# Linear attention on one core: the output of five of twelve groups written in 4 KB runs instead of 2 KB runs

## The chip, the cores and the metric

The kernel runs on one core of one Trainium2 chip. The metric is the device time of one execution in microseconds (us). Five runs of the kernel before took 127.0 to 128.05 us, median 127.46 us. A separate execution was profiled; its trace is what the views below show.

The names of the engines in the profile are PE (TensorE, matrix multiply), PEld (TensorE's weight loads), DVE (VectorE), ACT (ScalarE), POOL (GpSimd) and SP (SyncE, which here only issues transfers). "Sixteen DMA engines" are the engines that move the data; POOL and SP issue transfers to them through queues of their own.

## The reference, cut to what matters

Q, K and V are fp32 tensors of 8 x 12 heads, 512 rows and 64 columns.

```python
Q_feat = np.maximum(0, Q) + 1
K_feat = np.maximum(0, K) + 1
KV = np.einsum('bhkd,bhkv->bhdv', K_feat, V)            # 64 x 64 per head
K_sum = np.sum(K_feat, axis=2)                          # 64 per head
numerator = np.einsum('bhqd,bhdv->bhqv', Q_feat, KV)
denominator = np.einsum('bhqd,bhd->bhq', Q_feat, K_sum)
return numerator / (denominator[:, :, :, None] + 1e-10)
```

Inputs and output have 12.58 MB each, so 37.75 MB are read and 12.58 MB written.

## The kernel before, in words

**Layout of the inputs.** The 96 heads are taken in NG = 12 groups of eight. A group has two input blocks n. In a block, each of the 128 partitions holds C2 = 16 consecutive rows of 64 numbers, which is one run of 4 KB in memory, and 32 partitions make up one head. So a group is 2 blocks x 4 heads, and the 32 partitions 32b to 32b+31 belong to head b of each block. Loads go through POOL's queue and turn fp32 into bf16 on the way (all but the first K, which SP loads as fp32). Each K, V and Q load takes two groups (1024 KB in bf16) except for the first and the last ones, which take one.

**Steps of a group.** `k_features` and `q_features` add 1 and clip at 1 on VectorE. `v_blocks` copies V into a tile in which each head's rows stand apart (three copies on VectorE, one on ScalarE). `keys_values` makes KV and K_sum of the eight heads with 32 matmuls in two tiles of 64 columns, one tile for each block n, and ScalarE writes them as `kva`, a matrix of 128 x 130 for each b: block n = 0 in the upper 64 partitions and first 65 columns, block n = 1 in the rest, zeros elsewhere. `transposes` turns the Q features with 16 transposes, one for each row c of the 16 that a partition holds: the result has the 64 features of both blocks on its 128 partitions and the group's 128 row places as its columns. ScalarE copies it to `qt` in two halves of 8 rows.

**The output step.** `output` multiplies `qt` with `kva`. In the kernel before, each matmul takes 64 columns of weights: 32 row places of head b, and for each of them row c and row c + 8, which `qt` holds next to each other (`qt` is stored as row, place, half). Its 64 results therefore need 64 partitions, and a partition of the output holds 8 consecutive rows, a run of 2 KB. A pass h = 0, 1 handles heads 2h and 2h+1, one in each of the two 64-column tiles of TensorE. A pass fills two PSUM tiles `o_ps` (there are two buffers), eight matmuls each. For each `o_ps` VectorE takes the reciprocal of the denominators (L199) and multiplies (L200) into `o_sb`.

**Stores.** `store` sends one group's `o_sb`, 1024 KB. Groups 0 to 9 go through POOL as one transfer, groups 10 and 11 through SP as two transfers each, one per pass h, so that the first can go when pass 0 is done:

```python
o_dram = view(out, C)          # "(n p c) d -> p n c d" with c = 8: runs of 2 KB
...
if g < NG - 2:
    nc.gpsimd.dma_start(out=o_to, in_=o_sb)
    return
for h in range(2):
    nc.sync.dma_start(out=o_to[:, h:NP:2], in_=o_sb[:, h:NP:2])
```

**Order.** The order of all instructions is written out by hand. Each turn g of the main loop runs, on each engine's queue in this order: features of K, V's blocks, features of Q for group g; transposes of group g - 1; output of group g - 2; keys and values of group g; then a load two pairs ahead (every second turn), and the store of group g - 3. After the loop come group 11's steps, with output(9), output(10) and output(11), and the stores of groups 8 to 11. So POOL's queue holds loads and stores in one line, and TensorE's queue has, in each turn, transposes, output matmuls, key-value matmuls.

Of the kernel before, what the change touches and what calls it, by code (L numbers as in the profile page):

```python
# [8 lines left out]
FP32 = mybir.dt.float32  # L9
BF16 = mybir.dt.bfloat16  # L10
ALU = mybir.AluOpType

BANK = 512
# [6 lines left out]
def kernel(  # L20
# [18 lines left out]
    nc = tc.nc  # L39

    B, H, S, D = Q.shape
    P = 128
    C = 8
    C2 = 2 * C
    NPAIR = B * H * S // (P * C)
    NP = 4
    NG = NPAIR // NP
    D1 = D + 1
    W = 2 * D1

    def view(t, c):
        return t.flatten_outer_dims().rearrange("(n p c) d -> p n c d", p=P, c=c)
# [1 line left out]
    q_dram = view(Q, C2)  # L54
    k_dram = view(K, C2)
    v_dram = view(V, C2)
    o_dram = view(out, C)

    const = ctx.enter_context(tc.tile_pool(name="const", bufs=1))
    head_pool = ctx.enter_context(tc.tile_pool(name="head_pool", bufs=1))  # L60
# [2 lines left out]
    mid_pool = ctx.enter_context(tc.tile_pool(name="mid", bufs=3))  # L63
    out_pool = ctx.enter_context(tc.tile_pool(name="out_pool", bufs=OUT_BUFS))
    recip_pool = ctx.enter_context(tc.tile_pool(name="recip", bufs=4))
    psum_kva = ctx.enter_context(tc.tile_pool(name="psum_kva", bufs=2, space=bass.MemoryType.PSUM))
    psum = ctx.enter_context(tc.tile_pool(name="psum", bufs=2, space=bass.MemoryType.PSUM))
# [3 lines left out]
    NV = 3  # L71
# [4 lines left out]
    kva_diag = [const.tile([P, 4, 2, D1], BF16, name=f"kva_diag{i}") for i in range(NV)]  # L76
# [4 lines left out]
    qfs = {}  # L81
    qts = {}
    outs = {}

    def own(g):
        return slice(g % 2 * 2, g % 2 * 2 + 2)
# [24 lines left out]

    def store(g):
        o_sb = outs.pop(g)
        o_to = o_dram[:, g * NP : g * NP + NP]
        if g < NG - 2:
            nc.gpsimd.dma_start(out=o_to, in_=o_sb)  # L116
            return
        for h in range(2):
            nc.sync.dma_start(out=o_to[:, h:NP:2], in_=o_sb[:, h:NP:2])

    def feature(dst, src):
        nc.vector.tensor_scalar(  # L122
# [46 lines left out]

    def transposes(g):  # L170
        qf = qfs.pop(g)
        qt = mid_pool.tile([P, C, P, 2], BF16, name="qt")
        for half in range(2):
            qt_ps = psum_qt.tile([P, C, P], BF16, name="qt_ps")
            for c in range(C):
                nc.tensor.transpose(qt_ps[:, c, :], qf[:, half * C + c, :, :], identity)  # L176
            nc.scalar.copy(out=qt[:, :, :, half], in_=qt_ps)  # L177
        qts[g] = qt

    def output(g):  # L180
        kva = kva_diag[g % NV]
        qt = qts.pop(g)
        o_sb = out_pool.tile([P, NP, C, D], FP32, name="o_sb")
        for h in range(2):
            ops = [psum.tile([P, 2, BANK], FP32, tag="ps", name="o_ps") for _ in range(2)]
            for c in range(C):
                for j in range(2):
                    b = 2 * h + j
                    nc.tensor.matmul(  # L189
                        ops[c // 4][64 * j : 64 * j + 64, c // 2 % 2, (c % 2) * W : (c % 2) * W + W],  # L190
                        lhsT=qt[:, c, 32 * b : 32 * b + 32, :],
                        rhs=kva[:, b],
                        start=True,
                        stop=True,
                    )
            for i in range(2):
                cells = ops[i][:, :, 0 : 2 * W].rearrange("p b (c n x) -> p b c n x", n=2, x=D1)
                recip = recip_pool.tile([P, 2, 2, 2, 1], FP32, name="recip")
                nc.vector.reciprocal(out=recip, in_=cells[:, :, :, :, D:D1])  # L199
                nc.vector.tensor_tensor(  # L200
                    out=o_sb[:, h:NP:2, 4 * i : 4 * i + 4].rearrange(
                        "p n (b c) d -> p b c n d", b=2
                    ),
                    in0=cells[:, :, :, :, 0:D],
                    in1=recip.to_broadcast([P, 2, 2, 2, D]),
                    op=ALU.mult,
                )
        outs[g] = o_sb

    def clear(first, split, end):  # L210
# [7 lines left out]
    with tc.manual_schedule():  # L218
# [15 lines left out]
        for g in range(NG - 1):  # L234
            k_features(g)
            v_blocks(g)
            q_features(g)
            if g:
                transposes(g - 1)
            if g >= 2:  # L240
                output(g - 2)
            keys_values(g)
            if g % 2 and g // 2 + 2 < NG // 2:
                load_pair(g // 2 + 2)
            if g >= LAG:
                store(g - LAG)
        last = NG - 1
        k_features(last)
        v_blocks(last)
        transposes(last - 1)  # L250
        output(last - 2)
        q_features(last)
        keys_values(last)
        transposes(last)
        output(last - 1)
        output(last)
        for g in range(last - LAG, NG):
            store(g)
# [30 lines left out]
```

## Time and profile before

| | |
|---|---|
| median of five runs | 127.46 us (127.0 to 128.05) |
| profiled execution | 127.47 us, of which the profile's span is 125.7 us |
| busy, share of the span | DVE 88.4 us (70%), ACT 68.0 (54%), PE 66.7 (53%), PEld 49.9 (40%), POOL 27.5 (22%) |
| HBM | 37.75 MB read, 12.58 MB written, 400 GB/s over the span |
| output matmuls (L189) | 384, in tiles of 128 x 64 weights and 130 columns |
| reciprocal (L199), multiply (L200) | 48 of 199 ns, 48 of 692 ns |
| copy of the transposes (L177) | 24 of 1310 ns |
| store issues | POOL 10 of 1024 KB, SP 4 of 512 KB |

The busy times of engines overlap. A share of 70% for VectorE is an average over the span; it does not say whether VectorE sets the time. In the rows of 40 slices each slice is 3.14 us long; a digit is the busy share in tenths. The row GB/s counts the bytes that the DMA engines write. Times of instructions and transfers below are microseconds from the span's start.

### The profile page before, as it was taken

To read this page: it belongs to the slowest core of one execution; us is meant where nothing else is said; L and a number is where in the kernel's file an instruction comes from. 1 tells how busy PE (TensorE), PEld (TensorE's weight loads), DVE (VectorE), ACT (ScalarE), POOL (GpSimd) and SP (SyncE) were. 2 spreads that over 40 slices of the span, in tenths; PEclk is the share of its full clock that TensorE was granted. 3 is DMA by queue.
4 is the path that set the end of the run, shared out by engine and by line. 5 is a ranking of instruction groups with operands and counts; after the bars stand their busy time and mean duration, and the time that the engine had idled before them with its cause. 6 is when DMAs were issued, how large, how long until landed. Compare 5 with 4: busy or idle time off the path is not lost.

```text
span 125.7 us, 2337 instructions
## 1 busy us (share of the span) xinstructions
PE 66.7 (53%) x960; PEld 49.9 (40%) x960; DVE 88.4 (70%) x188; ACT 68.0 (54%) x87; POOL 27.5 (22%) x43
## 2 busy tenths in 40 slices
PE   0005959000059693895918967005978479694400
PEld 0004648000046482674706655004656357472200
DVE  4896280206199898999979892619969998849910
ACT  7832198007600989549791593760088962986000
POOL 6990213000002090024500160203222002020000
PEclk9999999965556999599997799855599968999855
DMA  4999999999999999999999999999999999999992
GB/s 85 330 213 209 211 211 212 211 209 214 211 211 214 211 211 213 211 211 214 247 413 295 198 211 212 212 352 393 214 211 211 213 271 415 417 420 411 403 402 96
DMA packets 13419, 32.13 MB, mean 256 GB/s; under 512 B 608, under 2 KB 608, under 8 KB 13408
## 3 DMA queue, kind: packets, MB, share of 16 engines
q0 software_dynamic: 12048, 28.84, 98.5%
q1 hardware_dynamic: 1360, 3.15, 6.9%
q8 instruction: 7, 0.11, 0.3%
q14 instruction: 4, 0.03, 0.1%
HBM read 37.75 MB, written 12.58 MB: 400 GB/s over the span
## 4 chain that ended last, share of the span: by engine, by line
DMA 53%; DVE 21%; PE 12%; issue 6%; POOL 3%; POOLq 0%; DVEq 0%
DMA q_raw<-in_Q_dram 44%; DVE o_sb L200 12%; DMA v_raw<-in_V_dram 10%; PE kva_ps L157 8%; DVE v_all L140 4%; DVE recip L199 2%; PE qt_ps L176 2%; PE o_ps L189 2%; POOL v_raw L99 2%; DVE qf L122 2%; DVE kf L122 1%; POOL q_raw L99 1%; POOL k_raw L99 0%; POOL zero L219 0%; POOLq L99 0%
## 5 line engine op out<-in xcount | busy, mean ns | idle before, releaser
L157 PE MATMUL kva_ps<-v_all,kf 128*64 128x320 bf16 x384 | 37.2, 361 | 12.2 <-DVE v_all L140 10.7
L189 PE MATMUL o_ps<-kva_diag,qt 128*64 128x130 bf16 x384 | 19.6, 238 | 39.7 <-DVE o_sb L200 39.2
L200 DVE TENSOR_TENSOR o_sb<-o_ps,recip 128x512 f32<-128x512 f32 x48 | 33.2, 692 | 1.6
L157 PEld LDWEIGHTS <-kf 128*64 128x64 bf16 x384 | 26.2, 135 | 19.8 <-DVE v_all L140 12.1
L140 DVE COPY v_all<-v_raw 32x2048 bf16<-32x2048 bf16 x36 | 26.5, 736 | 10.6 <-DMA v_raw<-in_V_dram 10.2
L189 PEld LDWEIGHTS <-qt 128*64 128x64 bf16 x384 | 13.0, 116 | 45.3 <-DVE o_sb L200 43.5
L177 ACT COPY qt<-qt_ps 128x1024 bf16<-128x1024 bf16 x24 | 29.7, 1310 | 0.3
L138 ACT COPY v_all<-v_raw 32x2048 bf16<-32x2048 bf16 x12 | 22.7, 1895 | 12.6 <-DMA v_raw<-in_V_dram 12.3
L167 ACT CAST kva_diag<-kva_ps 64x256 bf16<-64x256 f32 x24 | 8.9, 373 | 33.4 <-PE kva_ps L157 33.3
L122 DVE TENSOR_SCALAR qf<-q_raw 128x1024 bf16<-128x1024 bf16 x24 | 9.1, 423 | 7.0 <-DMA q_raw<-in_Q_dram 6.9
L99 POOL DMA_DIRECT2D k_raw<-in_K_dram x7 | 5.3, 755 | 38.2 <-DVE kf L122 38.2
L176 PE MATMUL qt_ps<-identity,qf 128*128 128x128 bf16 x192 | 13.4, 225 | 0.0
L122 DVE TENSOR_SCALAR kf<-k_raw 128x1024 bf16<-128x1024 bf16 x22 | 8.9, 447 | 6.0 <-DMA k_raw<-in_K_dram 6.0
L116 POOL DMA_DIRECT2D out_dram<-o_sb x10 | 8.2, 820 | 21.9 <-DVE o_sb L200 15.9
L176 PEld LDWEIGHTS <-qf 128*128 128x128 bf16 x192 | 11.4, 101 | 3.5 <-issue 3.3
L199 DVE RECIPROCAL recip<-o_ps 128x8 f32<-128x8 f32 x48 | 9.6, 199 | 4.1 <-PE o_ps L189 4.1
L99 POOL DMA_DIRECT2D v_raw<-in_V_dram x8 | 6.1, 760 | 19.3 <-ACT v_all L138 14.8
L99 POOL DMA_DIRECT2D q_raw<-in_Q_dram x8 | 5.9, 740 | 4.2 <-DMA q_raw<-in_Q_dram 4.2
L213 DVE MEMSET v_all<- 128x3072 f32 (+1 forms) x2 | 4.4, 2192 | 1.1 <-DVE ones L225 0.7
L168 ACT CAST kva_diag<-kva_ps 64x4 bf16<-64x4 f32 x24 | 4.0, 169 | 0.0
L214 ACT COPY v_all<-zero 128x2048 f32<-128x2048 f32 x2 | 3.7, 1896 | 0.0
L214 ACT ACT_TABLE_LOAD x1 | 1.3, 1283 | 0.7 <-PEq L273 0.7
(12 smaller groups left out, 4.6 us busy)
## 6 DMA issues: line engine op xcount, KB each, us to landing
out_dram<-o_sb POOLq DMA_DIRECT2D x10, 1024.0 KB, 19.9
k_raw<-in_K_dram POOLq DMA_DIRECT2D x4, 1024.0 KB, 18.2
v_raw<-in_V_dram POOLq DMA_DIRECT2D x4, 1024.0 KB, 21.2
q_raw<-in_Q_dram POOLq DMA_DIRECT2D x4, 1024.0 KB, 25.3
v_raw<-in_V_dram POOLq DMA_DIRECT2D x4, 512.0 KB, 16.6
q_raw<-in_Q_dram POOLq DMA_DIRECT2D x4, 512.0 KB, 16.9
out_dram<-o_sb SPq DMA_DIRECT2D x4, 512.0 KB, 5.5
k_raw<-in_K_dram POOLq DMA_DIRECT2D x3, 512.0 KB, 23.3
```

The costliest lines, as they stand in the source:

```text
L99: nc.gpsimd.dma_start(out=t[:, ms], in_=drams[x][:, 2 * groups[0] : 2 * groups[-1] + 2])
L116: nc.gpsimd.dma_start(out=o_to, in_=o_sb)
L122: nc.vector.tensor_scalar(out=dst, in0=src, scalar1=1.0, scalar2=1.0, op0=ALU.add, op1=ALU.max)
L138: nc.scalar.copy(out=v_blk[g % 2][ps, b], in_=v_raw[ps])
L140: nc.vector.tensor_copy(out=v_blk[g % 2][ps, b], in_=v_raw[ps])
L157: nc.tensor.matmul(kva_ps[64 * n : 64 * n + 64], lhsT=kf[:, c, n, :], rhs=vb[:, :, n, c, :], start=(c == 0), stop=(c == C2 - 1),)
L167: nc.scalar.copy(out=kva[ps, :, n, 0:D], in_=kva_ps[ps, sb : sb + 4, :])
L176: nc.tensor.transpose(qt_ps[:, c, :], qf[:, half * C + c, :, :], identity)
L177: nc.scalar.copy(out=qt[:, :, :, half], in_=qt_ps)
L189: nc.tensor.matmul(ops[c // 4][64 * j : 64 * j + 64, c // 2 % 2, (c % 2) * W : (c % 2) * W + W], lhsT=qt[:, c, 32 * b : 32 * b + 32, :], r ...
L199: nc.vector.reciprocal(out=recip, in_=cells[:, :, :, :, D:D1])
L200: nc.vector.tensor_tensor(out=o_sb[:, h:NP:2, 4 * i : 4 * i + 4].rearrange("p n (b c) d -> p b c n d", b=2), in0=cells[:, :, :, :, 0:D], i ...
```

## The change

For groups 6 to 10 (`in_quads`), the output is written in runs of 4 KB; the other groups keep 2 KB. In these five groups `qt` holds the 16 rows one after the other, and a matmul takes 32 columns of weights: the 32 row places of head b for one row c. Four matmuls, b = 0 to 3, stand in the four 32-column tiles of TensorE and fill the four quarters of an `o_ps` tile's partitions. An `o_ps` tile now holds four rows of all eight heads and needs 16 matmuls of 130 columns instead of 8; a group has 64 instead of 32. A partition of the output holds all 16 rows of its input block, 4 KB in one run. Reciprocal and multiply move to a function `normalise`, with shapes as before. Groups 6 to 9 are still one POOL transfer each. Group 10 is still two SP transfers, now one for each input block n instead of one for each pass h; each `o_ps` tile has a part in both.

```diff
-    o_dram = view(out, C)
+    o_pair = view(out, C)
+    o_quad = view(out, C2)
...
+    def in_quads(g):
+        return NG - 6 <= g < NG - 1
...
     def store(g):
         o_sb = outs.pop(g)
-        o_to = o_dram[:, g * NP : g * NP + NP]
+        to_quad = o_quad[:, 2 * g : 2 * g + 2]
+        to_pair = o_pair[:, g * NP : g * NP + NP]
         if g < NG - 2:
-            nc.gpsimd.dma_start(out=o_to, in_=o_sb)
-            return
-        for h in range(2):
-            nc.sync.dma_start(out=o_to[:, h:NP:2], in_=o_sb[:, h:NP:2])
+            nc.gpsimd.dma_start(out=to_quad if in_quads(g) else to_pair, in_=o_sb)
+        elif in_quads(g):
+            for n in range(2):
+                nc.sync.dma_start(out=to_quad[:, n], in_=o_sb[:, n])
+        else:
+            for h in range(2):
+                nc.sync.dma_start(out=to_pair[:, h:NP:2], in_=o_sb[:, h:NP:2])
...
     def transposes(g):
-        qt = mid_pool.tile([P, C, P, 2], BF16, name="qt")
+        qt = mid_pool.tile([P, C2 * P], BF16, name="qt")
+        qt_pair = qt.rearrange("p (c q r) -> p c q r", c=C, r=2)
+        qt_quad = qt.rearrange("p (c q) -> p c q", c=C2)
...
-            nc.scalar.copy(out=qt[:, :, :, half], in_=qt_ps)
+            to = qt_quad[:, half * C : half * C + C] if in_quads(g) else qt_pair[:, :, :, half]
+            nc.scalar.copy(out=to, in_=qt_ps)
...
+    def output_quads(g):
+        kva = kva_diag[g % NV]
+        qt = qts.pop(g)
+        o_sb = out_pool.tile([P, 2, C2, D], FP32, name="o_sb")
+        for i in range(4):
+            o_ps = psum.tile([P, 2, BANK], FP32, tag="ps", name="o_ps")
+            for c in range(4):
+                for b in range(4):
+                    bs = slice(32 * b, 32 * b + 32)
+                    nc.tensor.matmul(
+                        o_ps[bs, c // 2, (c % 2) * W : (c % 2) * W + W],
+                        lhsT=qt[:, 4 * i + c, bs],
+                        rhs=kva[:, b],
+                        start=True,
+                        stop=True,
+                    )
+            normalise(o_sb[:, :, 4 * i : 4 * i + 4], o_ps)
+        outs[g] = o_sb
```

More of the change, by code (lines that the diff above doesn't have):

```diff
@@ L176, in transposes, with normalise @@
                 nc.tensor.transpose(qt_ps[:, c, :], qf[:, half * C + c, :, :], identity)
-            nc.scalar.copy(out=qt[:, :, :, half], in_=qt_ps)
-        qts[g] = qt
+            to = qt_quad[:, half * C : half * C + C] if in_quads(g) else qt_pair[:, :, :, half]
+            nc.scalar.copy(out=to, in_=qt_ps)
+        qts[g] = qt_quad if in_quads(g) else qt_pair
+    def normalise(dst, o_ps):
+        cells = o_ps[:, :, 0 : 2 * W].rearrange("p b (c n x) -> p b c n x", n=2, x=D1)
+        recip = recip_pool.tile([P, 2, 2, 2, 1], FP32, name="recip")
+        nc.vector.reciprocal(out=recip, in_=cells[:, :, :, :, D:D1])
+        nc.vector.tensor_tensor(
+            out=dst.rearrange("p n (b c) d -> p b c n d", b=2),
+            in0=cells[:, :, :, :, 0:D],
+            in1=recip.to_broadcast([P, 2, 2, 2, D]),
+            op=ALU.mult,
+        )
[14 more added lines that the diff above has]
+                        stop=True,
+                    )
+            normalise(o_sb[:, :, 4 * i : 4 * i + 4], o_ps)
+        outs[g] = o_sb
     def output(g):
+        if in_quads(g):
+            output_quads(g)
+            return
         kva = kva_diag[g % NV]
@@ L196, in output @@
             for i in range(2):
[L197 to L207, printed above, removed]
+                normalise(o_sb[:, h:NP:2, 4 * i : 4 * i + 4], ops[i])
         outs[g] = o_sb
```

## The prediction

> **What bounds the kernel now.** I read the 40 slices and the queue table of the page first, then a table of stages cut at the last packets, then the chain of waits, then the timeline of TensorE and VectorE in the last 20 us, and at the end the trace's single DMA packets (one record each: queue, start, duration, bytes). The slices and queues:
>
> ```profile
> DVE  4896280206199898999979892619969998849910
> DMA  4999999999999999999999999999999999999992
> GB/s 85 330 213 209 211 211 212 211 209 214 211 211 214 211 211 213 211 211 214 247 413 295 198 211 212 212 352 393 214 211 211 213 271 415 417 420 411 403 402 96
> q0 software_dynamic: 12048, 28.84, 98.5%
> q1 hardware_dynamic: 1360, 3.15, 6.9%
> q8 instruction: 7, 0.11, 0.3%
> ```
>
> The 16 DMA engines are busy in every slice. The GB/s row counts bytes written: a load reads fp32 and writes bf16, so 211 there is 422 GB/s read from HBM. A store counts in full: 415 to 420. Both directions run at one rate, and no slice has a hole. The tail, in stages of one store each:
>
> ```profile
> core 0: us, PE busy (x) PEld busy (x) DVE busy (x) ACT busy (x) POOL busy (x), PEclk, DMA share, GB/s
> 104.50:107.00 2.50, 2.50 (x42) 1.92 (x40) 1.81 (x3) 1.09 (x5) 0.00 (x0) 0.94 1.02 419
> ...
> 112.00:114.50 2.50, 1.63 (x36) 1.20 (x33) 1.40 (x4) 2.46 (x6) 0.00 (x0) 1.00 1.02 411
> ...
> 117.00:119.50 2.50, 0.88 (x16) 0.51 (x16) 2.40 (x7) 0.00 (x0) 0.00 (x0) 0.79 1.02 399
> 119.50:122.00 2.50, 0.00 (x0) 0.00 (x0) 0.34 (x1) 0.00 (x0) 0.00 (x0) 0.50 1.05 404
> 122.00:123.00 1.00, 0.00 (x0) 0.00 (x0) 0.00 (x0) 0.00 (x0) 0.00 (x0) 0.50 0.88 342
> 123.00:124.00 1.00, 0.00 (x0) 0.00 (x0) 0.00 (x0) 0.00 (x0) 0.00 (x0) 0.50 0.41 160
> ```
>
> The last load's packets start by 104.1 us. From there on only stores run, back to back, and they are old work: nearly all of eight groups (4 to 11) is still to be written. From 122 on the share falls from 1.05 to 0.88 to 0.41: the 16 engines do not finish together. The packets show why. Each transfer ends on each engine with a 4-byte packet, so 16 of these time the engines apart. For the store of group 9 they stand at 116.94 us for the earliest engine and, behind it, at 0.29, 0.42, 0.45, 0.52, 0.88, 1.12, 1.17, 1.18, 1.19, 1.48, 1.88, 1.91, 1.93, 2.02 and 2.42. The latest one (119.36) then has its four SP stores left and sends its last packet at 124.35. **That one engine sets the end.** It never pauses, so compute matters only if a store reaches it too late.
>
> The chain of waits tells another story:
>
> ```profile
> DMA 53%; DVE 21%; PE 12%; issue 6%; POOL 3%; POOLq 0%; DVEq 0%
> ...
> 119.00 0.12 DVE recip L199
> 119.13 0.02 issue
> 119.15 0.69 DVE o_sb L200
> ```
>
> It ends at the last multiply (119.84), because the last store is issued then. But SP's four stores go out at 114.83, 116.51, 118.19 and 119.87, and the fastest engines, done at 122.2, begin the last of them by 120.9, so issue to packet takes about 1.0 us. The latest engine needs it only when it is done with three of its four: 119.36 + 3 x 1.28 = 123.2. Compute may end 2.3 us later before the end moves. The store of group 9 (POOL, issued 110.97, so ready at about 112) is reached by that engine at 116.77: 4.8 us to spare.
>
> **The change, part by part.** *Stores of groups 6 to 9 (POOL).* What can be saved is the difference between one 4 KB run and two 2 KB runs. In the trace two runs of a store already share one packet: 2560 packets of 4096 bytes for 5120 runs, median 159 ns. The packets of the first K load, which are single 4 KB runs, take the same median 159 ns. Back to back, a store of 16 packets per engine takes 2.49 us (155.6 ns a packet), a load of 32 packets, each reading one 4 KB run, 4.95 us (154.7 ns). If the new stores run like the loads, 0.9 ns x 64 packets = 0.06 us comes off the latest engine. I take -0.05; the bounds are 0.1 either way, the upper gain being the tail's mean packet (160.7) brought down to its median: 1.7 ns x 64.
>
> The Trainium skill (DMA: Bandwidth & Descriptors, Specifications) speaks against a gain: it puts full rate at 512 B and above, so 2 KB runs have nothing to win. The same table's 435 GB/s ceiling would, as an estimate, take 4 x 1.05 MB from 9.96 to 9.64 us, a gain of 0.32 us; the trace's loads already use 4 KB runs and stay at 422, so I leave that out.
>
> *Store of group 10 (SP).* Here each run is its own packet: 1024 of 2048 bytes, 84 ns, about 99.5 started per 0.5 us on 16 engines, 80.4 ns each. The group's 32 per engine take 2.57 us; as 16 packets of 4 KB at 155.6 ns, 2.49. This lies on the path: -0.08 us (0 to -0.15).
>
> The split of this store turns from output halves into input blocks n, and every multiply of the new output writes both n. So SP's first half, issued at 114.83 now, waits for the fourth multiply and goes at 116.51 with the second. Behind it on SP stand only the two stores of group 11, due at 118.19 and 119.87; two issues of 0.37 us fit between. Its packets are ready at about 117.5; the latest engine is on group 9's store until 119.3, so it loses nothing. The five engines that finish group 9 by 117.5 stand idle for up to 0.6 us, and being 1.9 us and more ahead at that point, they still end first. Cost 0, with 1.8 us of cover; without it, the lateness less that cover.
>
> *TensorE.* Five groups of 32 matmuls (128x64 weights, 130 columns) become five of 64 (128x32 weights): 160 more matmuls and as many weight loads. Now the two column tiles run together:
>
> ```profile
> 106.76 0.64 PE L189 MATMUL o_ps<-kva_diag,qt 128*64 128x130 bf16 x16
> 108.21 0.42 PE L189 MATMUL o_ps<-kva_diag,qt 128*64 128x130 bf16 x8 [0.81 <-DVE o_sb L200]
> 109.05 0.42 PE L189 MATMUL o_ps<-kva_diag,qt 128*64 128x130 bf16 x8 [0.42 <-DVE o_sb L200]
> ```
>
> Eight matmuls are four steps of 56.6 ns at full clock plus about 0.2 us to the end: 0.42 us. In single records the two matmuls of a step start 2 to 3 ns apart with the weight loads 2 ns behind them, so four should start within some 14 ns and the step stays one of 57 to 64 ns: a tile of o_ps still fills in 0.42 to 0.45. No 32-column tile runs in this trace. The bound above is that only two overlap: eight steps, 0.65 us, +0.23. Even that fits under the 0.84 us in which VectorE works off the other buffer (0.13 + 0.02 + 0.69), except at two places per group: the first fill after the transposes, which VectorE waits for, and the last one, behind which the next group's key-value matmuls are queued. At the bound that is 2 x 0.23 x 5 groups = 2.3 us on the compute chain, about the 2.3 us of cover: end +0. I take 0.1 us per group, hidden.
>
> The Trainium skill (TensorEngine Tiling (Array Packing), Instruction Overhead) has about 60 cycles for every matmul; at its 2.4 GHz that estimates 16 x 25 = 0.40 us for a fill's issue instead of 0.23, and still the cover holds. Starts 2 ns apart say the overhead is not paid between tiles.
>
> *ACT, VectorE, POOL.* The copy out of the transposes writes plain rows instead of every second element: 1024 elements in 1310 ns either way is my value; at 0.2 us less per copy nothing later would notice, since ACT is idle 46% of the span. Reciprocal (199 ns) and multiply (692 ns) keep shape, strides and count. POOL's store issue (768 ns with 512 runs, loads of 256 runs 720) is off the path with at least 4.8 us of cover.
>
> *Instruction blocks.* q8's seven packets are 16 KB each, about 950 ns, at 23, 48, 59, 70, 90, 100 and 113 us, when TensorE has run some 226, 522, 766, 965, 1262, 1508 and 1828 instructions: one block per 256. The change makes 1929 instructions 2249: one block more. Each block falls on one DMA engine and puts it back by about 1.0 us for good (after the first, one engine stands at 1.34 us where the rest are within 0.28; after the second, two; after the third, three, the last at 1.27). Every one I can follow hits an engine not hit before. So I expect the eighth on an engine not yet set back, at most 1.2 us behind, and 1.2 + 1.0 is still under 2.42: +0. Bounds 0 and +1.0.
>
> **Sum.** The profiled execution took 127.47 us (span 125.7, 1.8 around it), the median of the runs 127.46. -0.05 - 0.08 + 0 + 0 = -0.13: about 127.3.
>
> **The rivals.**
> *The extra instruction block lands on a late engine (slower).* It decides from 1.4 us behind the earliest: 6 of the 16 lags (1.48 to 2.42) qualify, with 0.06, 0.46, 0.49, 0.51, 0.60 and 1.0 us, mean 0.52: 127.85, at most 128.35. Against it: the hits seen went round. Chance 0.22.
> *TensorE becomes the bound (slower).* If four tiles do not overlap at all, a fill takes 16 x 56.6 ns + 0.2 = 1.1 us, +0.69. Twice per group exposed, plus 2 x 0.27 for the buffers waited for, 1.9 us x 5 = 9.6, less the cover of 2.3: +7 us, 134. A lesser case, cover just used up and 1 us over, is 128.5. It starts at 0.46 us of lateness per group. Against it: the 2 ns starts. Chance 0.13.
> *The late engine falls less far behind (faster).* Its lag grew by 0.68 us at 62 to 72 us and by 0.47 at 87 to 91, where stores and loads alternate. If new timing spares it one such step, 0.5 to 0.7 us go: 126.7. Against it: those stores are groups 0 to 3, which keep 2 KB runs, and from 92 us on the spread stays at 2.44. Chance 0.2.
> That 4 KB runs do not appear at all would leave 127.45, inside the main case.
>
> **How the numbers follow.** Main case 0.45, 126.95 to 127.7 by its bounds and the spread of the runs shown (127.0 to 128.05). Half a per cent, 0.64 us, is about what a measurement of this kernel tells from no change. Same: 0.38 of the main case, 0.08 of the block, 0.04 of the faster rival, 0.01 of TensorE's, 0.51. Slower: 0.03 + 0.14 + 0.12 = 0.29. Faster: 0.04 + 0.16 = 0.20. Range 126.6 to 128.7: it leaves out most of TensorE's case and the lower part of the faster one.
>
> **What would show it.** Right: POOL packets of four stores still at about 159 ns, 2.49 us per store; 512 SP packets of 2 KB and 256 of 4 KB at about 159 ns; SP's first two stores together near 116.5; a fill of 16 matmuls in 0.42 to 0.45 us; eight blocks on q8; last multiply near 120. Wrong: a hole in the DMA row after 104 us, a last multiply after 122, a spread of the engines that is not about 2.4 us, or 4 KB packets clearly off 159 ns.

## The result, and the profile after

The changed kernel took 127.69 us (median of 44 runs, 126.62 to 129.71), the kernel before 127.27 us (79 runs). The ratio of the compared runs is 1.0023, with a 95% interval of 1.0012 to 1.0035. So the change costs about 0.3 us by the ratio (0.4 by the medians). That is inside the half per cent that I called "same", but the forecast was a gain of 0.13 us, and the loss is clear of noise.

The profiled execution took 128.27 us: a span of 126.5 and 1.8 around it. First the slices and the queues:

```profile
DMA  3999999999999999999999999999999999999990
GB/s 74 339 211 210 210 211 214 210 210 214 211 210 214 211 211 213 211 212 212 273 416 264 202 212 212 222 377 361 214 210 214 209 322 414 414 418 414 408 346 34
...
q0 software_dynamic: 12048, 28.84, 97.7%
q1 hardware_dynamic: 1104, 3.15, 6.6%
q8 instruction: 9, 0.15, 0.4%
```

POOL's queue has the same number of packets as before, 12048: two 2 KB runs shared a packet, one 4 KB run fills it. SP's queue has 256 fewer (1104 for 1360): 512 of 2 KB have become 256 of 4 KB. q8 is the queue that fetches instructions, in blocks of 16 KB; it has nine blocks where before had seven, and I had expected eight. The tail, in the stages used before (busy time of the engines, granted clock, DMA share, GB/s), first one stage of before that was not shown yet, then the changed kernel:

```profile
107.00:109.50 2.50, 1.27 (x36) 0.92 (x32) 2.18 (x6) 2.48 (x2) 0.00 (x0) 1.00 1.03 419
```

```profile
107.00:109.50 2.50, 1.27 (x40) 0.92 (x42) 2.40 (x7) 2.48 (x3) 0.00 (x0) 1.00 1.02 416
...
112.00:114.50 2.50, 1.32 (x55) 0.86 (x52) 1.69 (x5) 2.48 (x4) 0.00 (x0) 1.00 1.03 415
...
117.00:119.50 2.50, 1.06 (x16) 0.66 (x16) 2.40 (x7) 0.00 (x0) 0.00 (x0) 0.65 1.02 410
119.50:122.00 2.50, 0.00 (x0) 0.00 (x0) 0.05 (x1) 0.00 (x0) 0.00 (x0) 0.50 1.01 395
122.00:123.00 1.00, 0.00 (x0) 0.00 (x0) 0.00 (x0) 0.00 (x0) 0.00 (x0) 0.50 0.85 317
123.00:124.00 1.00, 0.00 (x0) 0.00 (x0) 0.00 (x0) 0.00 (x0) 0.00 (x0) 0.50 0.34 129
```

The stores of groups 6 to 9 run from about 107 us on (106.84 us is the earliest end packet of group 5's store). The rates there are those of before: 415 to 419 GB/s with 4 KB runs in the four stages from 107 to 117 us, which had 411 to 419 with 2 KB. No hole shows in the DMA share. Most engines finish earlier than before (0.34 against 0.41 in the last stage), but a few packets follow until 125.19. TensorE and SP in the timeline (start, duration, instruction, count):

```profile
106.35 0.64 PE L211 MATMUL o_ps<-kva_diag,qt 128*32 128x130 bf16 x32
107.80 0.41 PE L211 MATMUL o_ps<-kva_diag,qt 128*32 128x130 bf16 x16 [0.81 <-DVE o_sb L195]
108.64 0.41 PE L211 MATMUL o_ps<-kva_diag,qt 128*32 128x130 bf16 x16 [0.43 <-DVE o_sb L195]
```

```profile
116.22 0.84 SPq L124 DMA_DIRECT2D out_dram<-o_sb  x2
117.90 2.06 SPq L127 DMA_DIRECT2D out_dram<-o_sb  x2
```

Sixteen matmuls in four column tiles fill an `o_ps` in 0.41 us, as eight in two tiles did in 0.42. SP's first two stores go together at 116.2. The last multiply ends at 119.55, 0.3 us earlier than before. Nothing here is late, except one thing, which the queue view of the last stretch (119 to 126.5 us) shows:

```profile
DMA  9899998999999988997855532211100000000000
...
q8 instruction: 1, 0.02, 0.8%
```

A block of instructions for TensorE is fetched at 121.3 us by the packet records, 2.7 us after the last matmul. It stands on an engine for 0.93 us, in the middle of SP's stores. In this execution the latest of all engines sends its last packet at 125.19, and the next at 124.50; the 0.7 us between them fit a block on an engine that was about 0.3 us ahead of the latest.

The eighth block cost something in this execution, too. In the last POOL stores the end packets come 2.49 us apart on each engine, so single engines can be followed. While the eighth block was fetched (112.7 us), one engine, 1.1 to 1.3 us behind the earliest, took 3.8 to 4.1 us for a store (two engines lie close together there, hence the ranges). From then on it stood 2.65 us behind, where the latest engine had been 2.16 behind: about 0.5 us more.

A single execution says little about an effect of 0.3 us. Each run lists its time and its span, and the difference is what lies outside the span. That number turned out to be the key: over the 130 runs of the kernel before, in the four comparisons below, it is 1.77 to 1.78 us on average and never above 1.85. In the changed kernel it is 2.03 on average, above 2.0 in 16 of 39 runs, and up to 2.87. (Five of the 44 runs, more than 1.5% above the fastest, are left out of the ratio and of these means as slow; four of them have 2.8 to 3.4 us outside as well, so the means rather understate the loss.) The span itself is 125.59 us on average, against 125.56 to 125.75 before.

### The profile page after: what moved, and what is told of

The parts are those of the page before. It is cut to its first block, busy times and chain, and to the rows that moved or that the text cites. A ratio compares the mean times of both kernels' runs of the same rounds, so it can differ in the third digit from the quotient of the medians.

```text
span 126.5 us, 2657 instructions
## 1 busy us (share of the span) xinstructions
PE 66.1 (52%) x1120; PEld 48.7 (38%) x1120; DVE 87.9 (69%) x188; ACT 65.3 (52%) x87; POOL 27.3 (22%) x43
## 3 DMA queue, kind: packets, MB, share of 16 engines
q0 software_dynamic: 12048, 28.84, 97.7%
q1 hardware_dynamic: 1104, 3.15, 6.6%
## 4 chain that ended last, share of the span: by engine, by line
DMA 54%; DVE 21%; PE 12%; issue 5%; POOL 3%; POOLq 0%; DVEq 0%
DMA q_raw<-in_Q_dram 44%; DVE o_sb L195 12%; DMA v_raw<-in_V_dram 9%; PE kva_ps L165 7%; DVE v_all L148 4%; DVE recip L194 2%; PE qt_ps L186 2%; PE o_ps L211 2%; POOL v_raw L103 2%; DVE qf L130 2%; DVE kf L130 1%; POOL q_raw L103 1%; POOL k_raw L103 0%; POOL zero L253 0%; POOLq L103 0%
## 5 line engine op out<-in xcount | busy, mean ns | idle before, releaser
L165 PE MATMUL kva_ps<-v_all,kf 128*64 128x320 bf16 x384 | 36.4, 356 | 12.6 <-DVE v_all L148 10.7
L165 PEld LDWEIGHTS <-kf 128*64 128x64 bf16 x384 | 25.4, 132 | 20.5 <-DVE v_all L148 12.4
L188 ACT COPY qt<-qt_ps 128x1024 bf16<-128x1024 bf16 x24 | 27.0, 1186 | 0.3
L233 PE MATMUL o_ps<-kva_diag,qt 128*64 128x130 bf16 x224 | 11.5, 237 | 27.0 <-DVE o_sb L195 26.5
L233 PEld LDWEIGHTS <-qt 128*64 128x64 bf16 x224 | 7.6, 116 | 30.3 <-DVE o_sb L195 29.0
L211 PE MATMUL o_ps<-kva_diag,qt 128*32 128x130 bf16 x320 | 8.2, 239 | 12.9 <-DVE o_sb L195 12.9
L211 PEld LDWEIGHTS <-qt 128*32 128x32 bf16 x320 | 5.1, 102 | 15.3 <-DVE o_sb L195 14.8
```

The source lines that it names most:

```text
L165: nc.tensor.matmul(kva_ps[64 * n : 64 * n + 64], lhsT=kf[:, c, n, :], rhs=vb[:, :, n, c, :], start=(c == 0), stop=(c == C2 - 1),)
L188: nc.scalar.copy(out=to, in_=qt_ps)
L211: nc.tensor.matmul(o_ps[bs, c // 2, (c % 2) * W : (c % 2) * W + W], lhsT=qt[:, 4 * i + c, bs], rhs=kva[:, b], start=True, stop=True,)
L233: nc.tensor.matmul(ops[c // 4][64 * j : 64 * j + 64, c // 2 % 2, (c % 2) * W : (c % 2) * W + W], lhsT=qt[:, c, 32 * b : 32 * b + 32, :], r ...
```

## The experiments

Some terms first. TensorE's *stream* is the list of its instructions: two for each matmul (weight load and matmul) and two more, 1922 before and 2242 after. (The prediction's 1929 and 2249 count seven more records; only differences matter here.) *Outside* is the time of a run less its span.

Two theories to begin with. The **block theory**: the two extra instruction blocks put DMA engines back. The **store theory**: the 4 KB runs, or the store of group 10 that SP holds back, cost the time. Each kernel was timed in five rounds beside the kernel before.

**Matmuls cut, stores as before (e1).** `in_parts(g)` is groups 6 to 10:

```diff
-                    nc.tensor.matmul(
-                        ops[c // 4][64 * j : 64 * j + 64, ...],
-                        lhsT=qt[:, c, 32 * b : 32 * b + 32, :],
+                    for u in range(2):           # in_parts(g)
+                        nc.tensor.matmul(
+                            ops[c // 4][64 * j + 32 * u : 64 * j + 32 * u + 32, ...],
+                            lhsT=qt[:, c, 32 * b + 16 * u : 32 * b + 16 * u + 16, :],
```

> The kernel before, its stores untouched (2 KB runs everywhere), with each output matmul of groups 6 to 10 cut into two of 32 columns: 160 more matmuls and 160 more weight loads, as in the change. Block theory (TensorE's two extra 16 KB instruction blocks put DMA engines back): 9 packets on q8 and the same loss as the change, a ratio of 1.001 to 1.004 to before. Store theory (the loss comes from the 4 KB runs or from SP's held-back first store): ratio 1.000 within 0.001.

Measured: 1.0023 (0.9999 to 1.0047), the loss of the change without any change to a store. Outside the span: 2.23 us on average, above 2.0 in 8 of 12 runs; span 125.69. In the profiled execution eight blocks lie inside the span of 125.8. This run has 2.65 us outside, a long ending. The ninth block comes after the span; the queue view from 125.8 to 130 us holds nothing else:

```profile
DMA  0000000000000000060000000000000000000000
...
DMA packets 1, 0.02 MB, mean 4 GB/s; under 512 B 0, under 2 KB 0, under 8 KB 0
...
q8 instruction: 1, 0.02, 1.6%
```

**The change with a stream as short as before (e2).**

```diff
-        for c in range(C2):
+        rows = range(0, C2, 2) if 1 <= g <= 10 else range(C2)
+        for c in rows:
```

> The changed kernel, stores and 32-column tiles kept, but the key-value matmuls of groups 1 to 10 take only every second row c (this leaves out half of the rows of K and V there): 160 matmuls and 160 weight loads fewer, so TensorE's stream is as long as in the kernel before. Block theory: 7 packets on q8 and a ratio of 0.998 to 1.000 to before. Store theory: the loss stays, 1.001 to 1.004.

Measured: 0.9954 (0.9930 to 0.9977), 1.79 us outside, span 125.22, seven blocks. The loss is gone, and more than expected. (The kernels with rows left out, e2, e5, e6 and f3, do not compute the whole result; they serve for timing alone.)

**Group 10's first store held back, nothing else (e3).**

```diff
+            ns = slice(2 * h, 2 * h + 2) if g == NG - 2 else slice(h, NP, 2)
-            nc.sync.dma_start(out=o_to[:, h:NP:2], in_=o_sb[:, h:NP:2])
+            nc.sync.dma_start(out=o_to[:, ns], in_=o_sb[:, ns])
```

> The kernel before with one edit: group 10's two SP stores are cut by block pairs (0,1 and 2,3) instead of by pass, still in 2 KB runs, so that the first waits for the fourth multiply and goes at about 116.5 us instead of 114.8. If the held-back store costs the change its time: 1.001 to 1.004, and idle on the late engines near 117.5 to 119. By the prediction's cover of 1.8 us and by the block theory: 1.000 within 0.001, 7 packets on q8.

Measured: 0.9985 (0.9958 to 1.0011), span 125.56, 1.78 outside. Holding the store back costs nothing that shows.

**All output and key-value matmuls cut in two (e4).** The cut of e1 in all groups, and the same for `keys_values`.

> The kernel before with every output matmul and every key-value matmul cut into two of 32 columns: 768 more matmuls and as many weight loads, a stream of some 3460 instructions instead of 1920. Block theory, exaggerated: 13 or 14 packets on q8, so nearly every engine is put back once by about 1.0 us, and the time rises by 0.5 to 1.5 us (1.004 to 1.012). Store theory: no change (1.000 within 0.002), since the fills keep their length and TensorE has cover.

Measured: 1.0041 (1.0015 to 1.0068), 13 blocks. The span rises to 126.35; outside it are 1.77 us on average and at most 1.81. So many blocks do cost, inside the span, but in another place than the change and e1.

**Two controls for e2 (e5, e6).** e5 is e1 with e2's rows left out; e6 is the kernel before with e2's rows left out.

> The kernel before with 2 KB runs throughout, the output matmuls of groups 6 to 10 cut into two of 32 columns, and the key-value matmuls of groups 1 to 10 taking every second row c (half of the rows of K and V left out there). Stream as long as before's, 7 blocks on q8; it differs from the last kernel that left these rows out (0.9954) only in its stores. If the 4 KB runs gave that kernel its gain: 0.999 to 1.001 here. If lighter key-value work gave it (TensorE reading less beside the DMA, or blocks fetched at better moments): 0.994 to 0.997 here too.

> The kernel before, 2 KB runs, 64-column tiles, with only the same half of the key-value matmuls of groups 1 to 10 left out: 320 instructions of TensorE fewer than before. Block theory: 5 or 6 packets on q8 and faster than before, 0.996 to 0.999, and 0.001 to 0.003 below the kernel of the same key-value work with seven blocks. Without an effect of blocks: equal to that kernel.

Measured: e5 0.9993 (0.9971 to 1.0015), span 125.66; e6 0.9985 (0.9962 to 1.0008), span 125.46, six blocks. Both have 1.78 to 1.80 us outside. One block more or less within seven is not resolved.

**Fewer groups in 4 KB runs (e7: group 10 alone; e8: groups 7 to 10).**

```diff
-        return NG - 6 <= g < NG - 1
+        return g == NG - 2              # e7
+        return NG - 5 <= g < NG - 1     # e8
```

> The changed kernel with only group 10 in 4 KB runs: 64 instructions of TensorE more than before, 1986, still short of an eighth block. SP's store of group 10 is held back and in 4 KB packets as in the change. Block theory: 7 blocks, 0.998 to 1.000 (0.08 us less for the SP packets). If the store of group 10 costs the time: 1.001 to 1.004.

> The changed kernel with groups 7 to 10 in 4 KB runs, group 6 in 2 KB: 2178 instructions of TensorE, 64 fewer than the change. Block theory: 8 packets on q8, none after 118 us, where the changed kernel had its ninth at 121.3 us; ratio 1.000 to 1.002, below the change's 1.0023 by the price of the last block. If the number of 4 KB stores set the loss instead: four fifths of 0.0023, 1.002.

Measured: e7 1.0038 (1.0009 to 1.0068), e8 0.9980 (0.9959 to 1.0002). **The block theory fails as I had put it:** e7, with fewer instructions than e8, is slower. The stores can't explain it either, since e1 has before's. What e7 shares with the change and with e1 is the end of TensorE's stream. It is 1986 instructions long, the other two 2242, and both are 194 past a multiple of 256, 62 short of the next block. And the loss lies outside the span: 2.15 us for e7, 1.79 for e8. In e7's profile the eighth block comes at 126.9 us, after the span of 125.9, though this run itself, with 1.9 us outside, is hardly longer than others. Hence a third theory, the **end-of-stream theory**: a stream that ends just short of a block boundary fetches one more block while the kernel ends, and the end waits for it.

**The end of the stream alone (f1, f2).** e1's cut for group 10 only, and for groups 9 and 10; stores as before.

> The kernel before with only group 10's output matmuls cut into two of 32 columns; all stores as before, 2 KB runs. TensorE's stream is 1986 instructions, 62 short of a multiple of 256, as in the changed kernel (2242). End-of-stream theory (a stream that ends just short of a block boundary fetches one more block while the kernel ends, and the end waits for it): the spans stay at 125.6 to 125.8 on average, the time outside the span rises from 1.78 to 2.1 to 2.3 us on average with about half of the runs above 2.0; ratio 1.002 to 1.004. Store theory and a theory of blocks counted inside the span (seven, as before): ratio 1.000, 1.78 us outside in every run.

> As the last one, but with groups 9 and 10 cut: 2050 instructions, two past the boundary at 2048, more than the last one and one block more. End-of-stream theory: the eighth block is fetched in the run of the stream, the time outside the span is 1.78 us in every run, ratio 0.999 to 1.001. If the number of matmuls or of blocks set the time: 1.002 to 1.005, no better than with group 10 alone.

Measured: f1 1.97 us outside on average, above 2.0 in 4 of 12 runs, up to 2.77; span 125.68. Its ratio, 1.0009 (0.9977 to 1.0042), does not decide, and the price is smaller than expected. f1's profiled run (2.06 us outside) shows no eighth block at all. f2, with 64 instructions more, has 1.78 us outside on average and at most 1.87, as expected; but its span is longer, 125.93, and its ratio is 1.0022 (0.9988 to 1.0057). Its eighth block comes at 117.3 us, in the last stores.

**The change with the end moved (f3, f4).** f3 is the change with e2's rows left out in groups 3 and 4 only; f4 is the change with group 11's matmuls cut as in e1.

> The changed kernel, all five groups in 4 KB runs, with every second row c left out of the key-value matmuls of groups 3 and 4 (half of the rows of K and V there): 64 instructions fewer, 2178. End-of-stream theory: outside the span 1.78 us in every run, spans of 125.5 to 125.7 on average as in the changed kernel, ratio 0.998 to 1.000. Store theory: 1.002 stays.

> The changed kernel, whole computation, with group 11's output matmuls cut into two of 32 columns as well (its stores stay in 2 KB runs): 64 instructions more, 2306, two past the boundary at 2304. End-of-stream theory: 1.78 us outside the span in every run; nine blocks in the span, the last near the end of the stream, where it can meet a late engine, so spans of 125.6 to 126.0; ratio 0.999 to 1.002. If longer streams cost in proportion: 1.003.

Measured: f3 0.9963 (0.9933 to 0.9994), 1.76 us outside, span 125.33: the long endings are gone. All five groups still write 4 KB runs there. f4 1.0054 (1.0026 to 1.0082): 1.80 outside, as expected, but a span of 126.35, well above what I had written. It has nine blocks inside the span, the last at 118.8 us.

**Do the 4 KB runs gain anything? (g1 to g3)** g1 is e8's twin with 2 KB runs (e1's cut in groups 7 to 10); g2 has groups 3 to 10 in 4 KB runs, g3 groups 6 to 9.

> The kernel before with the output matmuls of groups 7 to 10 cut into two of 32 columns, 2 KB runs throughout: 2178 instructions of TensorE, the twin of the kernel with groups 7 to 10 in 4 KB runs (span 125.43 on average, ratio 0.998). If the 4 KB runs shorten the span: 125.6 to 125.8 here, ratio 0.999 to 1.001. If the stream or its timing did it: 125.3 to 125.5, ratio 0.998.

> The changed kernel with groups 3 to 10 in 4 KB runs, whole computation, 2434 instructions of TensorE (130 past a block boundary, like before's 1922 and 2178). End-of-stream theory: 1.78 us outside the span in every run, nine blocks on q8, the last by about 115 us. If 4 KB runs shorten the span wherever they stand: 125.2 to 125.4, ratio 0.996 to 0.998. If only the late stores gain: 125.4, 0.998.

> The changed kernel with groups 6 to 9 in 4 KB runs and group 10 as before, 2178 instructions of TensorE, whole computation. SP's four stores are those of the kernel before. If POOL's 4 KB stores shorten the span: 125.3 to 125.5, ratio 0.997 to 0.999. If SP's store of group 10 does it: 125.6 to 125.8, ratio 0.999 to 1.001. Outside the span 1.78 us in every run by the end-of-stream theory.

Measured: g1 1.0007 (0.9982 to 1.0032), span 125.59. g3 1.0009 (0.9984 to 1.0034), span 125.62: POOL's four stores in 4 KB runs bring nothing. g2 1.0045 (1.0021 to 1.0069), span 126.27, nine blocks, 1.79 outside.

Side by side, ordered by what happens to the last block (means of 9 to 39 runs):

| kernel | stream, past a multiple of 256 | blocks inside the profiled span | span, us | outside, us | runs over 2.0 outside |
|---|---|---|---|---|---|
| before (130 runs) | 1922, 130 | 7 | 125.56 to 125.75 | 1.77 to 1.78 | 0 |
| e2, e3, e5 | 1922, 130 | 7 | 125.22, 125.56, 125.66 | 1.79, 1.78, 1.78 | 0 of 33 |
| e6 | 1602, 66 | 6 | 125.46 | 1.80 | 0 of 12 |
| e8, f3, g1, g3 | 2178, 130 | 8 | 125.43, 125.33, 125.59, 125.62 | 1.76 to 1.79 | 0 of 48 |
| f1, e7 | 1986, 194 | 7 | 125.68, 125.79 | 1.97, 2.15 | 9 of 24 |
| change, e1 | 2242, 194 | 9, 8 | 125.59, 125.69 | 2.03, 2.23 | 24 of 51 |
| f2 | 2050, 2 | 8 | 125.93 | 1.78 | 0 of 12 |
| f4, g2, e4 | 2306, 2434, 3458 | 9, 9, 13 | 126.35, 126.27, 126.35 | 1.77 to 1.80 | 0 of 36 |

The rows of f1, e7, the change and e1 hold 33 long endings in 75 runs. All other rows hold none in 271. The four kernels differ in stores, in the number of groups cut and in the number of blocks; they share the 194. The blocks themselves follow the length of the stream: a first block after 226 of TensorE's records (the count in most profiles) and one more for every 256 gives the 6, 7, 8, 9 and 13 of the table, but for the ninth block of the change. By this count the four kernels with the 194 end 25 records before the next block is due.

The nine-block kernels lose inside the span. The last stretches of e8 (eight blocks) and f4 (nine), from 122 us on:

```profile
122.00:123.00 1.00, 0.00 (x0) 0.00 (x0) 0.00 (x0) 0.00 (x0) 0.00 (x0) 0.50 0.99 383
123.00:124.00 1.00, 0.00 (x0) 0.00 (x0) 0.00 (x0) 0.00 (x0) 0.00 (x0) 0.50 0.56 209
124.00:125.00 1.00, 0.00 (x0) 0.00 (x0) 0.00 (x0) 0.00 (x0) 0.00 (x0) 0.50 0.00 0
```

```profile
122.00:123.00 1.00, 0.00 (x0) 0.00 (x0) 0.00 (x0) 0.00 (x0) 0.00 (x0) 0.50 0.99 383
123.00:124.00 1.00, 0.00 (x0) 0.00 (x0) 0.00 (x0) 0.00 (x0) 0.00 (x0) 0.50 0.62 231
124.00:125.00 1.00, 0.00 (x0) 0.00 (x0) 0.00 (x0) 0.00 (x0) 0.00 (x0) 0.50 0.07 27
```

Up to 124 they are nearly alike. After that e8 is done, and f4 has a share of 0.07 for 1 us, which is about one of sixteen engines still at work. The 4-byte end packets of the last store say it in numbers: in f4 the last engine is 1.59 us behind the first and the one before it 0.31; in g2 1.46 and 0.73; in e8 the last is only 0.30 behind the first. In f4 and g2 one late engine carries the loss. In g2 it can be followed to the block: for the store in which the ninth block falls (115.6 us) one engine took about 3.8 to 4.0 us instead of 2.49, and it is the last to finish group 9's store, 0.73 us behind the next. In e4, with 13 blocks, two engines end together, 1.97 and 1.99 us behind the first.

## Why the prediction was right or wrong, point by point

**What bounds the kernel: right.** The DMA engines run through, and the latest of them sets the end of the span. Compute had room: in e8 and f3 SP's last store was issued at 120.6 and 120.5 us instead of 119.9, and their spans are no longer than before's. f4 and e8 show the role of a single engine directly.

**Stores of groups 6 to 9: right.** 159 ns a packet before and after, one store every 2.49 us in the end packets; g3 finds no gain (1.0009, 0.9984 to 1.0034). The rule that I cited from the Trainium skill (DMA: Bandwidth & Descriptors, Specifications), full rate from 512 B on, agrees with that; but POOL's packets had 4096 bytes both times, so no packet of 2 KB was compared here.

**Store of group 10: size not settled.** SP's packets became what I said, 256 of 4 KB at a median of 159 ns. Kernels with this store and no late block (e2, e8, f3) have mean spans of 125.2 to 125.4 us, those without it (e3, e5, e6, g1, g3) 125.5 to 125.7. That is in the direction of the predicted 0.08 us and somewhat more. The pair made to decide it, e8 and g1, gives 0.9980 and 1.0007 with intervals that overlap. The end packets point the same way: from the last engine's end of group 9's store to the end of all stores it takes 5.07 us in each of the five kernels with the 4 KB store and no block in that stretch (e2, e7, e8, f3, g2), and 5.14 in e3, f1 and g3 with 2 KB. But the other 2 KB kernels without a block there take 3.94 to 5.06, before among them (5.06), and why is not shown. The hold-back costs nothing that shows (e3), though its cover of 1.8 us shrank where compute ended later: in e8 SP issues at 117.24, and the share drops to 0.79 from 117.5 to 118.5.

**TensorE: right.** A fill takes 0.41 us with four tiles; even 1536 cut matmuls in e4 left compute off the path. The estimate from the Trainium skill (TensorEngine Tiling (Array Packing), Instruction Overhead), 0.40 us of issue for 16 matmuls, is not seen: the whole fill, with some 0.2 us of latency, takes 0.41.

**ACT: the value was wrong, and without effect.** I took 1310 ns for both forms of the copy:

```profile
L188 ACT COPY qt<-qt_ps 128x1024 bf16<-128x1024 bf16 x24 | 27.0, 1186 | 0.3
```

Fourteen copies at 1310 ns leave (24 x 1186 - 14 x 1310) / 10 = 1012 ns for the ten with plain rows, 0.3 us less each; the single records show 1012 to 1018.

**Instruction blocks: here the prediction failed.** The step was "one block more ... +0", together with the last line of the sum, which carried the 1.8 us around the span over unchanged. Both halves went wrong. The change fetches two blocks more, not one: the eighth in the middle of the stores, as foreseen, and a ninth at the very end. The eighth has no visible price on average (e8, f3, g1 and g3 have eight, and spans no longer than before's). But the reason given for its +0 did not hold in the profiled execution: it fell on an engine about as little behind as foreseen (1.1 to 1.3 us), but set it back by 1.3 us or more instead of 1.0, past the latest one. The streams that end where the change's ends cost it 0.26 us on average outside the span (2.03 for 1.77), where the forecast had no term at all. The gain of 0.13 us that I expected inside the span stays within its scatter: 125.59 against 125.56 to 125.75. My threshold was off too: I counted up to the boundary at 2304 and found the stream (2242) below it. Ending 62 instructions short was not enough; 126 short (a remainder of 130) was.

The Trainium skill (Runtime: NRT & Kernel Launch, Instruction fetch mechanics) calls the cost of crossing a block boundary mostly hidden. For the first eight blocks the runs mostly agree (f2, at 125.93, is open); for a stream that ends close to a boundary they do not, by 0.2 to 0.45 us on average (1.97 to 2.23 outside, for 1.78).

**The rivals.** "The extra block lands on a late engine" named the right object and, for the change, mostly the wrong place. In the profiled execution the last two blocks did make engines the latest, and cost about 0.5 and 0.7 us. As a rule of the kernel it appears from nine blocks inside the span on (f4, g2, e4: 126.3 us). I had seen the first blocks go to engines not hit before and extended that to all. Nine and thirteen blocks give the same span, which would fit a round of eight engines, in which the ninth block meets the first one's engine again; the records do not name engines, so this is argued and not shown. f2, with eight blocks and the last at 117.3 us, lies between (125.93), and why is open. TensorE as the bound and a shorter lag through 4 KB runs did not show in the change.

**What stays open.** That the end of the stream makes the long endings is shown by the runs. That the end waits for a block is argued: one profiled run (e1) has both the late block and the long ending; e7's has the late block with a normal ending, f1's, with 2.06 us just over the line, has no late block on record. Only 33 of these kernels' 75 runs end long, and what decides it is unknown. In some executions, such as the profiled one of the change, the block comes inside the span instead; what decides that was not tried. Only remainders of 2, 66, 130 and 194 were run, so where exactly the zone begins is unknown. The kernel with groups 7 to 10 in 4 KB runs computes everything, has neither cost, and may beat both (0.9980, 0.9959 to 1.0002); that is not clear of noise.

## What to carry to other kernels

Count an engine's instructions as a resource of its own: code arrives in blocks of 256, each block's packet takes about 1 us of one DMA engine, and a stream that ends shortly before a block boundary (62 instructions here) can lengthen the end of the kernel. In a kernel bound by DMA, time the sixteen engines apart by their end packets, because the latest one sets the end and an average share hides it. And compare the time outside the span as well as the span: a profile that shows nothing slower is not yet a kernel that is not slower.

## What the runs showed of the hardware that I had not expected

- The time outside the span is not a constant of the kernel's kind. It is 1.72 to 1.91 us in 271 runs and up to 3.4 in the four kernels whose TensorE stream ends 62 instructions short of a block.
- Two 2 KB runs of a POOL store travel in one 4096-byte packet (159 ns); on SP's queue each 2 KB run is a packet of its own (84 ns, 80.4 from start to start).
- ScalarE's copy of 1024 bf16 elements out of PSUM takes 1310 ns when it writes every second element and 1012 to 1018 ns when it writes them in a row.
- Matmuls of 32 columns in four column tiles overlap fully at 130 columns: 16 fill their tile in 0.41 us, as fast as 8 of 64 columns in two.
